# Moving side work between the stages of a tuned decoder step: spatial product, softplus and first units

## The chip, the cores and the metric

The kernel runs on one core of a Trainium2 chip. The metric is the device time of one execution in microseconds (us), the median of several runs. The profile is of one execution; its times are counted from the start of its span.

The engines: TensorE (PE in rows; its weight loads are PEld), VectorE (DVE), ScalarE (ACT), GpSimd (POOL) and SyncE (SP), whose queue issues nearly all transfers (SPq). Each engine does its instructions in the order in which they stand in its queue, and an instruction that waits holds up all behind it.

## The reference

One layer of a gated decoder block for 1024 prompt tokens and 8 sample tokens, model width 1024, float32:

```
h = rmsnorm(x) * (1 + scale) + shift
u, v, g_a, x_b, g_b, z_a, z_b = split(h @ w_in)        # seven blocks of 1024 columns
v = rmsnorm(v) * v_norm_g                               # the sample rows of v are an output
y_a = u * (tril(w_s) @ v + b_s) * silu(g_a)             # in chunks of 128 tokens: the spatial product
xc = causal_conv(x_b)                                   # width 4
r, i = sigmoid(blockdiag(xc) + b)                       # the gates
log_a = -8 * r * softplus(-lam); a = exp(log_a)
y_b = scan(a, sqrt(1 - a*a) * i * xc) * silu(g_b)       # h_t = a h_{t-1} + x_t
out = x + gate * ((sigmoid(z_a) * (y_a @ w_pa) + sigmoid(z_b) * (y_b @ w_pb)) @ w_out)
```

and a last rmsnorm. `softplus(-lam)` is one value per channel, 1024 in all, and does not depend on the input x.

## The kernel before, in words

Each float32 factor is split into a high part (rounded to the matmul format) and a low part, and a product is three matmuls: high by high, high by low, low by high. The high part of a weight is made on ScalarE and the low part on VectorE (`split`).

The work is in four parts. The first makes h and, in tiles of 128 tokens by 512 columns, v (`v_tile`, `v_mm`). `v_evac` copies a v tile out of PSUM on VectorE, squares it on ScalarE for the norm, and stores the copy to DRAM (`vd`). The last tile of v, token block 3 and half 1, is computed after the sums of h that the second part needs (`x_forms`).

The second part is 23 units of seven stages: R (x_b, g_b: recurrent branch), Z (z_a, z_b) and G (u, g_a). The order is R0, Z0, Z1 and then rounds of three, R(i), G(i-1), Z(i+1), and at the end G7. A unit computes two blocks of 128 output columns by seven products (`FORMS` p1 to p7, in the first unit in the order p1, p4, p2, p6, p5, p7, p3), each a stage of 24 matmuls on TensorE (`seven`). The sums of h that they need are made once, and the sums of weights in `sums` on GpSimd. `unit` issues for each stage: the matmuls, the evacuation of the stage before (`evac`, from the list `later`), the weight split two stages ahead (`ahead(.., prep)`), the weight sums four stages ahead (`ahead(.., sums)`), and then the side work that stands in `side` for that stage. In the rows a unit's banks are called `a_R`, `b_R` and so on, its weight halves `wf_R0p`; p1 is copied out to `s_R`, p6 plus p1 to `u_R`.

Side work is put down with `at(stage, function, ...)`: the recurrent branch of unit R(i) (`recurrent`: convolution, gates, scan), and the spatial product for group g (`spatial`): load v, scale it by the norm, split it (`v_hi`, `v_lo`: tiles `vnh`, `vnl`), and two halves of the product (`sp_mm`), each 16 matmuls and, one stage later, its evacuation `fin` on VectorE. `n` in `spatial` is the first stage of G(g), so `n - 4` is the fourth stage of the R unit ahead of it. `do_rgconsts` and `spatial_consts` make small constants between the v tiles and the first unit, the softplus among them.

What sets the order on each queue: the tile framework lists instructions by priority, which is their place in the program, and by when its own model takes them for ready. `tc.high_priority(offset=400)` gives a block the priority of 400 instructions earlier. Where `in_order[0]` is set, every instruction of an engine wrapper (`V`, `A`, `TE`, `G`, `S`) is pinned behind the one traced before it on its engine. It is set for most of the first part and for the units from the second one on; the first unit, R0, is left to the framework's list. `tc.issue_after(x)` pins a block behind the instruction x.

The third part multiplies y_a and y_b by w_pa and w_pb, and the fourth is the product with w_out, the residual and the last norm.

The lines that the change touches: `v_evac` (L668), the sample row's gain (L727), the prefetch in `unit` (L936), the softplus in `do_rgconsts` (L1156 to L1177), the calls ahead of the units (L1440), `spatial` (L1506) and the loop over the units (L1527).

Of the kernel before, what the change touches and what calls it, by code (L numbers as in the profile page):

```python
# [10 lines left out]
AF = mybir.ActivationFunctionType  # L11
ALU = mybir.AluOpType

P = 128
# [10 lines left out]
HD = 512  # L25
# [28 lines left out]
def tile_hybrid_step(  # L54
# [102 lines left out]
        A.activation(hi, src, AF.Copy)  # L157
        (eng or V).tensor_tensor(lo, src, hi.bitcast(F32), ALU.subtract)

    last_w, last_a = [None], [None]  # L160

    def load_raw(name, shape, parts):
        raw = wst[0].tile(shape, F32, tag="raw", name=f"raw_{name}", bufs=4)
# [501 lines left out]
    ssv = ctile([P, NT, 2], "ssv")  # L665
    vd = drm.tile([NP, D], F32, tag="vd", name="vd")

    def v_evac(tt, half, ps):  # L668
        st = half_tile(f"vst{tt}_{half}")[:, 0:HD]
        V.tensor_copy(st, ps)  # L670
        last_a[0] = A.activation(
            junk[:, 0:HD], ps, AF.Square, accum_out=ssv[:, tt, half : half + 1]
        ).ins
        nc.sync.dma_start(out=vd[tt * P : (tt + 1) * P, half * HD : (half + 1) * HD], in_=st)

    vsr = slot("vsr", [P, D])[0:NS]
# [1 line left out]
    def v_tile(tt, half):  # L678
        ps = bank(f"v{tt}_{half}")
        for k in range(KT):  # L680
            if tt < NT:
                ht = h[k, tt // 4]
                tok_mm(ps, (ht[:, 0], ht[:, 1]), wv[k, half], k, P, tok(tt), h0s)
            else:
                packed_mm(ps, hsp, wv[k, half], k, h0s)
        if tt < NT:
            v_evac(tt, half, ps)
        else:
            unpack(vsr[:, half * HD : (half + 1) * HD], ps, NS)

# [33 lines left out]
    with tc.issue_after(last_w[0]):  # L724
        nc.sync.dma_start(out=vgb, in_=v_norm_g[0].partition_broadcast(NS))
    A.activation(vsr, vsr, AF.Copy, scale=rvs)
    V.tensor_tensor(vsr, vsr, vgb, ALU.mult)  # L727
    nc.sync.dma_start(out=chunk_v_sample[0, :, 0, :], in_=vsr)

    for tt in (5, 6, 7):  # L730
# [159 lines left out]
    def ahead(n, step):  # L890
        if n < len(stages):
            step(*stages[n])

    def unit(n0, u, use):
# [33 lines left out]
        for j, f in enumerate(FIRST if first else FORMS):  # L928
            bank_of = {"p1": pa_, "p2": pa_, "p6": pb_, "p7": pb_, "p4": pd_, "p5": pc_, "p3": pc_}
            now = later[:]  # L930
            later.clear()
            seven(u, f, bank_of[f], f in ("p1", "p6", "p5") or (first and f == "p4"))
            for step in now:
                step()
            later.append(lambda f=f: evac(f))
            ahead(n0 + j + 2, prep)  # L936
            ahead(n0 + j + 4, sums)
            for step in side.get(n0 + j, ()):
                step()
# [200 lines left out]
    def do_rgconsts():  # L1140
        pss = consts_pair[:, 1]
        A.activation(sth, pss[:, 0:256], AF.Copy)
        stv = sth[:, 64:256].rearrange("p (b w k) -> p w k b", b=NS, w=3)
        def taps(off):
            return (
                vec[:, off : off + KT].rearrange("p (k o) -> p k o", o=1).broadcast_to([P, KT, NS])
            )

        V.tensor_tensor(pre, stv[:, 0], taps(V_CW), ALU.mult)
        for k in (1, 2):  # L1150
            V.tensor_tensor(stv[:, k], stv[:, k], taps(V_CW + 8 * k), ALU.mult)
        V.tensor_tensor(pre, pre, taps(V_CB), ALU.add)
        for k in (1, 2):
            V.tensor_tensor(pre, pre, stv[:, k], ALU.add)

        lamv = vec[:, V_LAM : V_LAM + KT]  # L1156
        le = ctile([P, KT], "le")
        with tc.issue_after(last_a[0]):
            A.activation(le, lamv, AF.Abs)
        A.activation(le, le, AF.Exp, scale=-1.0)  # L1160
        l1 = ctile([P, KT], "l1")
        V.tensor_scalar(l1, le, 2.0, None, ALU.add)
        V.reciprocal(l1, l1)
        V.tensor_tensor(l1, l1, le, ALU.mult)
        l2 = ctile([P, KT], "l2")
        V.tensor_tensor(l2, l1, l1, ALU.mult)
        l3 = ctile([P, KT], "l3")
        V.tensor_scalar(l3, l2, 1.0 / 15, 1.0 / 13, ALU.mult, ALU.add)
        for n in (11, 9, 7, 5, 3, 1):
            V.tensor_tensor(l3, l3, l2, ALU.mult)  # L1170
            V.tensor_scalar(l3, l3, 1.0 / n, None, ALU.add)
        V.tensor_tensor(l3, l3, l1, ALU.mult)
        V.tensor_scalar(l3, l3, 2.0, None, ALU.mult)
        V.tensor_scalar(l2, lamv, -1.0, 0.0, ALU.mult, ALU.max)
        V.tensor_tensor(l3, l3, l2, ALU.add)
        V.tensor_scalar(crg, l3, C_RG, None, ALU.mult)
        V.tensor_scalar(ncrg, l3, -C_RG, None, ALU.mult)  # L1177

    rgw = {}

# [256 lines left out]
        x_forms(kp)  # L1437
    for n in range(4):
        ahead(n, sums)
    for n in range(2):  # L1440
        ahead(n, prep)
    v_tile(3, 1)
    x_forms(3)
# [54 lines left out]
    def spatial(g, n):  # L1498

        at(n - 9, v_load, g)  # L1500
        at(n - 7, v_mask, g)
        at(n - 7, v_wst, g)
        at(n - 7, v_scale, g)
        at(n - 6, v_hi, g)
        at(n - 5, v_lo, g)
        at(n - 4, sp_mm, g, 0)  # L1506
        at(n - 3, sp_mm, g, 1)

    for i in range(KT):
        recurrent(i)  # L1510
        spatial(i, pos["G", i] + 5 * (i + 1 == KT))
        for step in range(3):
            at(pos["Z", i] + 5 + step, z_late, i, step)
# [10 lines left out]

    users = {"R": use_r, "Z": use_z, "G": use_g}
    for n, u in enumerate(units):
        if n == 1:  # L1527
            in_order[0] = True
        if n + 1 < len(units):
            load_unit(units[n + 1])  # L1530
        unit(7 * n, u, users[u[0]](u[1]))
# [154 lines left out]
```

## Time and profile before

| | |
|---|---|
| three runs | 978.2, 975.4, 978.35 us (median 978.2) |
| the profiled execution | 975.57 us, its span 973.9 us |
| TensorE busy | 940.3 us |
| VectorE busy | 642.0 us |
| ScalarE busy | 499.9 us |
| GpSimd busy | 223.5 us |
| mean granted TensorE clock | 0.996 of full speed |

A busy time is the sum of an engine's instructions. TensorE is the engine that has next to no idle time, so a wait of TensorE is time of the kernel, and work of the other engines matters where TensorE waits for it. A row of a timeline is a run of like instructions: start, length, engine, operation, output and inputs, shapes, count, and in brackets how long the engine stood idle ahead of it and what ended that. The length of a run of matmuls has the fill of the array in it, so one run overlaps the next by some 0.15 us. Nearly all instructions are recorded at line 45, the wrapper that issues them, so tiles and not lines tell them apart.

### The profile page before, as it was taken

The page shows a single profiled execution, that of the slowest core. Times are in us where ns is not written, and L with a number is a line of the kernel's source. Part 1 is how long each engine was busy: PE and PEld are TensorE (multiplying, and loading weights), DVE is VectorE, ACT ScalarE, POOL GpSimd, SP SyncE. Part 2 cuts the span into 40 slices and gives each one's busy share as a digit, 9 for nine tenths or more (in the row PEclk, how much of TensorE's full clock was granted, in tenths as well). Part 3 has the DMA queues.
Part 4 walks back from the last instruction along what each step waited for, and adds up shares of the span by engine and source line. Part 5 has one row for each costly group of instructions (what it writes and reads, how often), then busy time and mean ns, then how long its engine had stood idle before and what let it go on. Part 6 is the DMA issues. An engine that isn't in the chain of part 4 may idle for free. (4 is left out here: it accounts for less than half of the span.)

```text
span 973.9 us, 16564 instructions
## 1 busy us (share of the span) xinstructions
PE 940.3 (97%) x6575; PEld 877.6 (90%) x6575; DVE 642.0 (66%) x973; ACT 499.9 (51%) x809; POOL 223.5 (23%) x169
## 2 busy tenths in 40 slices
PE   7999997999999999999999999999999999999996
PEld 3778777999999999999999999999999999998785
DVE  3886887569578587695784875868534366555544
ACT  4674544684774855846748558467322133232212
POOL 1143432232232243342322433322000000000001
PEclk9999999999999999999999999999999999999999
DMA  9953112143143153241430621607875565424321
GB/s 288 292 169 106 67 36 64 48 141 110 44 139 115 35 165 97 80 152 44 139 93 23 185 69 51 183 23 257 283 271 193 174 213 180 152 93 167 110 71 62
DMA packets 127943, 126.27 MB, mean 130 GB/s; under 512 B 10503, under 2 KB 105279, under 8 KB 127857
## 3 DMA queue, kind: packets, MB, share of 16 engines
q1 hardware_dynamic: 126648, 120.96, 38.9%
q0 software_dynamic: 1216, 4.24, 1.3%
q8 instruction: 52, 0.85, 0.4%
q14 instruction: 27, 0.21, 0.1%
HBM read 93.92 MB, written 31.33 MB: 129 GB/s over the span
## 5 line engine op out<-in xcount | busy, mean ns | idle before, releaser
L45 PE MATMUL v<-wv,h 128*128 128x512 f32 x384 | 97.1, 401 | 2.8 <-ACT junk L45 1.7
L45 PE MATMUL ps_pb<-ybh,pb 128*128 128x344 f32 x384 | 91.0, 320 | 1.0 <-DVE pb L45 0.9
L45 PE MATMUL ps_pa<-yah,pa 128*128 128x344 f32 x384 | 91.4, 320 | 0.0
L45 PEld LDWEIGHTS v<-wv,h 128*128 128x128 f32 x384 | 69.6, 188 | 20.7 <-ACT junk L45 2.2
L45 POOL TENSOR_TENSOR rs_o<-ms_o,nhalf 128x1 f32<-128x1 f32 (+1 forms) x9 | 8.1, 894 | 296.6 <-DVE ms_o L45 296.6
L45 PEld LDWEIGHTS ps_pb<-ybh,pb 128*128 128x128 f32 x384 | 66.2, 188 | 1.5 <-DVE pb L45 1.2
L45 PEld LDWEIGHTS ps_pa<-yah,pa 128*128 128x128 f32 x384 | 66.6, 188 | 0.5
L45 PE MATMUL ps_pb<-ybl,pb 128*128 128x344 f32 x192 | 61.5, 320 | 1.5 <-DVE ybl L45 1.5
L45 PE MATMUL ps_pa<-yal,pa 128*128 128x344 f32 x192 | 61.5, 320 | 0.0
L45 PE MATMUL o<-woh,mgh 128*128 128x512 f32 x128 | 50.5, 395 | 0.0
L45 PE MATMUL o<-woh,mgl 128*128 128x512 f32 x128 | 50.5, 395 | 0.0
L45 PE MATMUL o<-wol,mgh 128*128 128x512 f32 x128 | 50.4, 394 | 0.0
L45 DVE SCALAR_TENSOR_TENSOR xc<-xb,vec,xc 128x512 f32<-128x512 f32 x48 | 48.2, 1005 | 0.6
L45 ACT ACT_TABLE_LOAD x34 | 43.6, 1283 | 1.4 <-PEq L1670 0.8
L45 ACT ACTIVATE mgh<-sa 128x344 fp32r<-128x344 f32 x24 | 11.7, 490 | 63.2 <-DVE sa L45 59.3
L45 DVE TENSOR_TENSOR sb<-ps_pb,sb 128x344 f32<-128x344 f32 x24 | 12.4, 515 | 46.0 <-PE ps_pb L45 46.0
L45 ACT ACTIVATE junk<-xr 128x512 bf16<-128x512 f32 (+2 forms) x19 | 11.6, 608 | 56.8 <-DVE xr L45 51.4
L45 POOL TENSOR_TENSOR wt_R<-raw_R,raw_R 128x512 f32<-128x512 f32 x8 | 16.9, 2106 | 95.4 <-DVE wf_Z5p L45 13.7
L45 PEld LDWEIGHTS ps_pb<-ybl,pb 128*128 128x128 f32 x192 | 36.0, 188 | 2.1 <-DVE ybl L45 2.1
L45 PEld LDWEIGHTS ps_pa<-yal,pa 128*128 128x128 f32 x192 | 36.1, 188 | 0.2
L45 POOL TENSOR_TENSOR wt_G<-raw_G,raw_G 128x512 f32<-128x512 f32 x8 | 14.0, 1755 | 92.9 <-DVE wf_G6p L45 13.9
L45 POOL TENSOR_TENSOR wt_R<-raw_R,wt_R 128x512 f32<-128x512 f32 x15 | 33.1, 2207 | 8.6 <-DVE wf_R6p L45 1.1
(535 smaller groups left out, 2543.3 us busy)
## 6 DMA issues: line engine op xcount, KB each, us to landing
raw_ada<-in_w_ada_dram SPq DMA_DIRECT2D x32, 256.0 KB
raw_R<-in_w_in_dram SPq DMA_DIRECT2D x16, 512.0 KB
raw_Z<-in_w_in_dram SPq DMA_DIRECT2D x16, 512.0 KB
raw_G<-in_w_in_dram SPq DMA_DIRECT2D x16, 512.0 KB
zad<-za SPq DMA_DIRECT2D x16, 258.0 KB
yad<-t SPq DMA_DIRECT2D x8, 516.0 KB
sb<-zbd SPq DMA_DIRECT2D x8, 516.0 KB
yar<-yad SPq DMA_DIRECT2D x8, 516.0 KB
```

What stands on the lines that cost most here:

```text
L45: ins = f(*args, **kwargs)
```

## The change

The spatial product's two halves go from stages n - 4 and n - 3 to n - 3 and n - 2, and with them their evacuations. The softplus is taken out of `do_rgconsts` and put down as side work in five pieces: its ScalarE operations, with a Sigmoid on a scratch tile behind them, in the first unit's third stage, and four groups of VectorE operations in stages 10 to 13, which are the last four of Z0. `in_order` is set from the first unit on. The weight split of R0's third stage is put ahead of the last v tile. The evacuations in `v_tile` get the priority of 400 instructions earlier. The product of the sample row of v with its gain goes from VectorE to GpSimd.

```diff
@@ -157,7 +157,7 @@
         A.activation(hi, src, AF.Copy)
         (eng or V).tensor_tensor(lo, src, hi.bitcast(F32), ALU.subtract)
 
-    last_w, last_a = [None], [None]
+    last_w = [None]
 
     def load_raw(name, shape, parts):
         raw = wst[0].tile(shape, F32, tag="raw", name=f"raw_{name}", bufs=4)
@@ -665,12 +665,11 @@
     ssv = ctile([P, NT, 2], "ssv")
     vd = drm.tile([NP, D], F32, tag="vd", name="vd")
 
-    def v_evac(tt, half, ps):
+    def v_evac(tt, half, ps, late=False):
         st = half_tile(f"vst{tt}_{half}")[:, 0:HD]
-        V.tensor_copy(st, ps)
-        last_a[0] = A.activation(
-            junk[:, 0:HD], ps, AF.Square, accum_out=ssv[:, tt, half : half + 1]
-        ).ins
+        with tc.high_priority(offset=400 if late else 0):
+            V.tensor_copy(st, ps)
+            A.activation(junk[:, 0:HD], ps, AF.Square, accum_out=ssv[:, tt, half : half + 1])
         nc.sync.dma_start(out=vd[tt * P : (tt + 1) * P, half * HD : (half + 1) * HD], in_=st)
 
     vsr = slot("vsr", [P, D])[0:NS]
@@ -684,7 +683,7 @@
             else:
                 packed_mm(ps, hsp, wv[k, half], k, h0s)
         if tt < NT:
-            v_evac(tt, half, ps)
+            v_evac(tt, half, ps, True)
         else:
             unpack(vsr[:, half * HD : (half + 1) * HD], ps, NS)
 
@@ -724,7 +723,7 @@
     with tc.issue_after(last_w[0]):
         nc.sync.dma_start(out=vgb, in_=v_norm_g[0].partition_broadcast(NS))
     A.activation(vsr, vsr, AF.Copy, scale=rvs)
-    V.tensor_tensor(vsr, vsr, vgb, ALU.mult)
+    G.tensor_tensor(vsr, vsr, vgb, ALU.mult)
     nc.sync.dma_start(out=chunk_v_sample[0, :, 0, :], in_=vsr)
 
     for tt in (5, 6, 7):
@@ -933,7 +932,8 @@
             for step in now:
                 step()
             later.append(lambda f=f: evac(f))
-            ahead(n0 + j + 2, prep)
+            if n0 + j > 0:
+                ahead(n0 + j + 2, prep)
             ahead(n0 + j + 4, sums)
             for step in side.get(n0 + j, ()):
                 step()
@@ -1153,28 +1153,31 @@
         for k in (1, 2):
             V.tensor_tensor(pre, pre, stv[:, k], ALU.add)
 
-        lamv = vec[:, V_LAM : V_LAM + KT]
-        le = ctile([P, KT], "le")
-        with tc.issue_after(last_a[0]):
+    lamv = vec[:, V_LAM : V_LAM + KT]
+    le, l1, l2, l3 = (ctile([P, KT], n) for n in ("le", "l1", "l2", "l3"))
+
+    def softplus(step):
+        if step < 0:
             A.activation(le, lamv, AF.Abs)
-        A.activation(le, le, AF.Exp, scale=-1.0)
-        l1 = ctile([P, KT], "l1")
-        V.tensor_scalar(l1, le, 2.0, None, ALU.add)
-        V.reciprocal(l1, l1)
-        V.tensor_tensor(l1, l1, le, ALU.mult)
-        l2 = ctile([P, KT], "l2")
-        V.tensor_tensor(l2, l1, l1, ALU.mult)
-        l3 = ctile([P, KT], "l3")
-        V.tensor_scalar(l3, l2, 1.0 / 15, 1.0 / 13, ALU.mult, ALU.add)
-        for n in (11, 9, 7, 5, 3, 1):
-            V.tensor_tensor(l3, l3, l2, ALU.mult)
-            V.tensor_scalar(l3, l3, 1.0 / n, None, ALU.add)
-        V.tensor_tensor(l3, l3, l1, ALU.mult)
-        V.tensor_scalar(l3, l3, 2.0, None, ALU.mult)
-        V.tensor_scalar(l2, lamv, -1.0, 0.0, ALU.mult, ALU.max)
-        V.tensor_tensor(l3, l3, l2, ALU.add)
-        V.tensor_scalar(crg, l3, C_RG, None, ALU.mult)
-        V.tensor_scalar(ncrg, l3, -C_RG, None, ALU.mult)
+            A.activation(le, le, AF.Exp, scale=-1.0)
+            A.activation(pre_act, nhalf, AF.Sigmoid)
+        elif step == 0:
+            V.tensor_scalar(l1, le, 2.0, None, ALU.add)
+            V.reciprocal(l1, l1)
+            V.tensor_tensor(l1, l1, le, ALU.mult)
+            V.tensor_tensor(l2, l1, l1, ALU.mult)
+            V.tensor_scalar(l3, l2, 1.0 / 15, 1.0 / 13, ALU.mult, ALU.add)
+        elif step < 3:
+            for n in ((11, 9, 7), (5, 3, 1))[step - 1]:
+                V.tensor_tensor(l3, l3, l2, ALU.mult)
+                V.tensor_scalar(l3, l3, 1.0 / n, None, ALU.add)
+        else:
+            V.tensor_tensor(l3, l3, l1, ALU.mult)
+            V.tensor_scalar(l3, l3, 2.0, None, ALU.mult)
+            V.tensor_scalar(l2, lamv, -1.0, 0.0, ALU.mult, ALU.max)
+            V.tensor_tensor(l3, l3, l2, ALU.add)
+            V.tensor_scalar(crg, l3, C_RG, None, ALU.mult)
+            V.tensor_scalar(ncrg, l3, -C_RG, None, ALU.mult)
 
     rgw = {}
 
@@ -1437,7 +1440,7 @@
         x_forms(kp)
     for n in range(4):
         ahead(n, sums)
-    for n in range(2):
+    for n in range(3):
         ahead(n, prep)
     v_tile(3, 1)
     x_forms(3)
@@ -1503,9 +1506,12 @@
         at(n - 7, v_scale, g)
         at(n - 6, v_hi, g)
         at(n - 5, v_lo, g)
-        at(n - 4, sp_mm, g, 0)
-        at(n - 3, sp_mm, g, 1)
-
+        at(n - 3, sp_mm, g, 0)
+        at(n - 2, sp_mm, g, 1)
+
+    at(2, softplus, -1)
+    for step in range(4):
+        at(10 + step, softplus, step)
     for i in range(KT):
         recurrent(i)
         spatial(i, pos["G", i] + 5 * (i + 1 == KT))
@@ -1524,7 +1530,7 @@
 
     users = {"R": use_r, "Z": use_z, "G": use_g}
     for n, u in enumerate(units):
-        if n == 1:
+        if n == 0:
             in_order[0] = True
         if n + 1 < len(units):
             load_unit(units[n + 1])
```

## Rows read from the trace of the kernel before

**Rows 1.** the page: busy time of each engine, share of the span, instructions

```profile
PE 940.3 (97%) x6575; PEld 877.6 (90%) x6575; DVE 642.0 (66%) x973; ACT 499.9 (51%) x809; POOL 223.5 (23%) x169
```

**Rows 2.** waits of TensorE: in total, times, longest (us)

```profile
PE sp L45 <- DVE vnl L45: 9.7, 7, 1.4
...
PE b_R L45 <- ACT u_R L45: 3.7, 1, 3.7
```

**Rows 3.** timeline of TensorE, last v tile to Z0: start, us, what

```profile
136.95 5.85 PE L45 MATMUL v<-wv,h 128*128 128x512 f32 x24 [1.73 <-ACT junk L45]
...
143.97 3.12 PE L45 MATMUL a_R<-h,wf_R0p 128*128 128x258 f32 x24
...
151.62 3.13 PE L45 MATMUL a_R<-h,wf_R0p 128*128 128x258 f32 x24 [1.65 <-ACT s_R L45]
...
164.16 4.58 PE L45 MATMUL b_R<-S,wf_R0p 128*128 128x258 f32 x24 [3.70 <-ACT u_R L45]
...
168.58 3.03 PE L45 MATMUL c_R<-S,wf_R0p 128*128 128x258 f32 x24
...
171.45 3.03 PE L45 MATMUL a_Z<-h,wf_Z0p 128*128 128x258 f32 x24
```

**Rows 4.** stretches: busy (x count) by engine, granted clock, DMA share, GB/s

```profile
164.00:166.00 2.00, 1.84 (x8) 1.84 (x9) 1.42 (x3) 1.11 (x3) 0.00 (x0) 0.50 0.29 84
...
196.00:198.00 2.00, 2.00 (x19) 2.00 (x18) 0.69 (x1) 2.00 (x4) 0.00 (x0) 1.00 0.32 122
```

**Rows 5.** timeline of VectorE, last v tiles and R0

```profile
127.48 4.89 DVE L45 TENSOR_TENSOR vsr<-vsr,vgb 8x1024 f32<-8x1024 f32 x1 [1.64 <-ACT vsr L45]
...
152.41 0.17 DVE L45 TENSOR_SCALAR l<-le 128x8 f32<-128x8 f32 x1
...
158.74 0.16 DVE L45 TENSOR_SCALAR ncrg<-l 128x8 f32<-128x8 f32 x1
...
162.78 0.69 DVE L45 TENSOR_TENSOR b_R<-b_R,s_R 128x516 f32<-128x516 f32 x1
```

**Rows 6.** timeline of GpSimd, last v tiles and R0

```profile
126.24 3.80 POOL L45 TENSOR_TENSOR f<-h 128x516 f32<-128x516 f32 x3
...
130.01 1.28 POOL L45 TENSOR_TENSOR wt<-raw_R,wt_R 128x512 f32<-128x512 f32 x1
...
150.58 1.72 POOL L45 TENSOR_TENSOR rs_v<-ms_v,nhalf 128x8 f32<-128x8 f32 x1 [9.71 <-DVE ms_v L45]
```

**Rows 7.** timeline of VectorE, units R3 and G2

```profile
357.43 1.22 DVE L45 TENSOR_TENSOR vnl<-vg,vnh 128x1024 fp32r<-128x1024 f32 x1
...
359.75 0.75 DVE L45 SCALAR_TENSOR_TENSOR t<-sp,vgc,wsr 128x512 f32<-128x512 f32 x1 [0.50 <-PE sp L45]
...
371.79 0.68 DVE L45 TENSOR_TENSOR wf_G2p<-wt_G,wf_G2p 128x512 fp32r<-128x512 f32 x1
```

**Rows 8.** timeline of ScalarE, R0

```profile
149.58 1.28 ACT L45 ACT_TABLE_LOAD   x1
...
150.99 0.58 ACT L45 ACTIVATE s_R<-a_R 128x516 f32<-128x516 f32 x1
```

**Rows 9.** timeline of the SP queue: transfers issued

```profile
145.87 2.52 SPq L45 DMA_DIRECT2D rgw<-in_w_rg_x_dram  x4
...
190.33 1.14 SPq L45 DMA_DIRECT2D raw_R<-in_w_in_dram  x2
```

**Rows 10.** timeline of TensorE, units R3 and G2

```profile
357.03 0.28 PE L45 MATMUL sp<-wsb,vnh 128*128 128x256 f32 x1
...
359.55 3.09 PE L45 MATMUL b_R<-S,wf_R3p 128*128 128x258 f32 x24
...
362.48 0.29 PE L45 MATMUL sp<-wsb,vnh 128*128 128x256 f32 x1
...
363.35 3.09 PE L45 MATMUL c_R<-S,wf_R3p 128*128 128x258 f32 x24
...
374.88 3.02 PE L45 MATMUL c_G<-S,wf_G2p 128*128 128x258 f32 x24
```

## The prediction

> **What bounds the kernel now.** I read the page's busy times first. TensorE is busy for 940.3 of the 973.9 us [rows 1], so what a reordering can give is in the 34 us in which it is not, and in stretches where its clock is low. The list of TensorE's waits comes next: one group, the spatial product waiting for the low part of v (`vnl`), has 9.7 us in 7 waits of up to 1.4, and the longest single wait is 3.7 us for the copy `u_R` [rows 2]. The timeline of TensorE at the first unit shows where the others lie: 1.73 us ahead of the last v tile, 1.65 us ahead of R0's third stage, and the 3.70 us ahead of its sixth [rows 3]. The windows then show what the long one costs besides: right behind it the granted clock is 0.50, the lower level (1.2 of 2.4 GHz), where it was 1.00 [rows 4].
>
> Everything the change touches is in these two places. Waits are priced from start to start, because a matmul's row also has the fill of the pipe in it and an idle array must be filled again.
>
> **The first unit.** From the start of p1 (143.97) to the start of Z0 (171.45) R0's seven stages take 27.48 us [rows 3]. An undisturbed stage takes 171.45 - 168.58 = 2.87 us, so seven take 20.1. The difference, 7.4, is the two waits (5.35), 1.55 from the sixth stage at the low clock (4.42 from 164.16 to 168.58, less 2.87), and refilling. With the 1.73 ahead of the v tile there is 9.1 us to be had. What ends each wait:
>
> - 1.73: the v tile takes the banks of an earlier v tile, whose evacuation is behind VectorE's product of the sample row with the gain, 4.89 us long [rows 5]. It ended at 132.37, 1.08 after GpSimd's run of sums ended (131.29) [rows 6]; the low part `vnl`, as long a row on 128 partitions, takes 1.22 [rows 7]. So 3.7 of the 4.89 was waiting for GpSimd. The change takes the product off VectorE, and the priority of 400 puts the copy and the square of a late v tile ahead of the sums of h (`x_forms`). On GpSimd the product costs about 2.5: three sums of 516 took 3.80 [rows 6], 1.27 each, and it has 1024. Its upper bound is the 4.89 it took on VectorE, its lower one the 1.22. I take 2.5, scaled from its own engine. Behind it on GpSimd are one to three form sums and `wt4`; these end at some 134 in place of 131.3, and their first reader that TensorE needs is p4's weight, at 145. It is hidden; without that cover it would cost its 2.5 once.
> - 1.65: ScalarE did the softplus's table load (1.28 at 149.58) before the copy `s_R` (150.99) [rows 8], though p1 had ended by 147.1. In program order `s_R` comes behind p4's matmuls and ahead of the softplus, so it can go right when p1 ends, 3 us before p2 asks.
> - 3.70 and the clock: the sum `b_R + s_R` ran at 162.78, though p5 had ended at 160.46 (164.16 less the 3.70) and p6 a stage ahead of it, by 157.6. VectorE first did the rest of the 23 small softplus operations, which run from 152.41 to 158.90 [rows 5], and then weight halves and convolution taps. In program order the sum stands behind one weight half.
>
> What is late next, in the new order: TensorE starts p1 at 142.2, then p4 at 145.2, p2 148.1, p6 150.9, p5 153.8, p7 156.7, Z0 162.4. ScalarE has, behind p4's end (148.1): a copy and a weight half to 149.3, then the softplus head with two table loads (one for Exp, one to preload Sigmoid). A load and the Exp behind it take 1.41 until `s_R` starts [rows 8], so the head is over by 152.4. Then p2's copies, p7's weight half (ends 153.8), its low part on VectorE (0.68 [rows 7]) to 154.5, the sum of p6 (0.69 [rows 5]) to 155.2, the copy `u_R` to 155.8. p7 asks at 156.7: 0.9 us to spare, the tightest place of the unit.
>
> The new pins add waits too. VectorE's first operation of unit 0 must follow the copy of the v norms, which waits for GpSimd's power, 1.72 [rows 6]; that hangs on the square of the last v tile, now near 142.8 (135.2 + 5.9 for the tile, 0.7 each for the copy and the square and a little more), so the norms' copy is done near 145. Behind it is p6's weight half, which p6 needs at 150.9: 4 us of cover at least. GpSimd's sum for p7's weight, once made early, is now pinned behind that power: ready near 146.4, wanted near 153. On SP the load of Z0's weights, earlier issued far ahead, is now pinned behind R0's eight small gate loads, whose last four ended issuing at 148.4 [rows 9]. Two loads of 512 KB each issued at 190.33 took 1.14 to issue, and the transfers had thinned out to 0.32 by 196 to 198 [rows 4, 9]; so Z0's weights land by some 156, and its first half is wanted on ScalarE at about 157.4, on TensorE at 162.4. Covered by 4 us against TensorE. The four softplus steps on VectorE lie in Z0's last four stages, 6.5 / 23 x 6 = 1.7 us each at most by the rows, and end a stage ahead of the tanh that reads them; TensorE shows no wait in that stretch. The weight half of p2 is prepared ahead of the last v tile and no more in stage 0: the same two operations, earlier.
>
> For the unit: 9.1, lower bound 0 (the waits only change names), upper bound 9.1.
>
> At the table loads the trace and a rule part. By the rows a switch is paid with 1.41, Exp included. The Trainium skill, "ScalarE: Activation LUTs", section "What ACT_TABLE_LOAD costs", gives about 2.66 us for every switch, a drain of about 1.38 behind the load. The two switches would by that be 2.5 us dearer, p7 would wait about 1.6, and the gain of the unit would be about 7.5; the row does not show such a drain, so I go by the row.
>
> **The rounds.** In R3, the round I take for all seven, the first spatial product starts at 357.03 and the stage behind it at 359.55, 2.52 us later; the second one takes 363.35 - 362.48 = 0.87 [rows 10]. So the wait costs 1.65 a round, a little more than the 1.40 that is listed, and 7 x 1.65 = 11.5 us. `vnl` is ready at 358.65 [rows 7]. One stage later the product comes behind p7, at 357.03 + 2.87 = 359.9: 1.25 us after `vnl`, and TensorE does not wait.
>
> What moves with it on VectorE: the two evacuations of the product, four operations of 0.75 [rows 7] and a short one, 3.2 us a round, each one stage later, into the stages with the convolution. Their readers, the G unit's products, are two stages off or more; in the last unit too, where the first half is used one stage after it is written. VectorE has no gap from 359.75 to the weight half that ends at 372.47, and p5 of G starts at 374.88 [rows 7, 10]: 2.41 to spare. TensorE now comes 1.65 earlier, and VectorE gets back the half microsecond that it stood idle ahead of the first evacuation, so some 1.3 us is left. I cost the move at nothing; if that cover is gone, up to 3.0 a round. At the end of the last G the second evacuation falls in front of the scan's inputs; that is between nothing and 1.5 us, and I take nothing, as in the rounds.
>
> **Sum.** 9.1 + 11.5 = 20.6 us. The profiled execution took 975.57 us, 1.67 over its span: 975.57 - 20.6 = 955.0. The three runs are 978.2, 975.4 and 978.35, so the median lies 2.6 above the profiled one; for the median of the new kernel I add half of that: 956.3.
>
> **The rivals.**
>
> - First unit: the waits change their names. The pinned queues put each engine's work behind whatever waits longest (the norms' copy on VectorE, the softplus head on ScalarE), and TensorE stands about as long as before at p6 or p7. Only the 1.73 stays: 956.3 + 7.4 = 963.7. For it: 0.9 us to spare at p7. Against: VectorE is freed of the 4.89 and of most of the 6.5 in this stretch.
> - The priority and the move to GpSimd change nothing at the v tile, because another operation is put first. 956.3 + 1.7 = 958.0.
> - Dear table loads hold up `u_R`: if each of the two switches kept ScalarE for twice the load's 1.28 [rows 8], that is 2.6 more, less the 0.9 to spare: 956.3 + 1.7 = 958.0. Against it is the 1.41 to `s_R`. The section of the Trainium skill on ScalarE named above speaks for it.
> - VectorE becomes late in the rounds: all 3.0 us of moved work fall ahead of p5's weight half, which had 1.3 to spare. A wait of 1.7 a round takes the place of the 1.65; the rounds give nothing: 956.3 + 11.9 = 968.2.
> - Slower: the same VectorE paces the stretch, the 3.0 us come through in full, and the clock falls in each round as it did behind the 3.70 (it stayed at 1.00 at the waits of 1.4). 3.0 + 1.55 = 4.55 a round, 31.9 in all: 956.3 + 31.9 = 988.2. It decides at 20.6 / 7 = 2.9 us of loss a round. The unbroken VectorE stretch speaks for it, the 1.3 us against it.
> - Neither place gains, since something untraced holds TensorE: about 976.
>
> **How the numbers follow.** Chances: forecast 0.60, v tile 0.07, table loads 0.03, first unit 0.14, rounds 0.10, slower 0.03, nothing 0.03. The likeliest case alone: 953.5 to 959. The range: down to 952.5, if runs sit at the profiled level (955.0) and the last G gives another 1.5 or a little more; up to 967, which takes in the unit's rival and most of the rounds' one. About 0.3% (2.9 us) is what can be told from no change here. Slower by more: 0.03; within: 0.03; faster: 0.94.
>
> **What would show it.** After: the list of TensorE's waits has neither `sp` for `vnl` nor `a_R` and `b_R` in R0; the granted clock is 1.00 in R0; p1 of R0 to Z0 takes about 20.2 us; a round from one R to the next is 1.65 shorter. Wrong steps would show as waits of R0 for `u_R` or a weight half, of p5 in G for a weight half, of the gate matmuls for the convolution's halves, or of the last v tile for the square. The forecast fails if any of these repeats in seven rounds.

## The result, and the profile after

The changed kernel takes 968.31 us (median of 965.57, 968.35, 968.27 and 968.96), the kernel before it, run beside it, 976.82 (four runs, 975.4 to 978.35): ratio 0.9907, 95% interval [0.9879, 0.9935]. It is faster by 8.5 us and not by 20.6; 956.3 was forecast, and 968.31 lies outside the range of 952.5 to 967. The profiled execution took 965.57 us, the least of the four, and its span went from 973.9 to 963.9.

Start to start on TensorE, the 10.0 us divide as follows (v3 is the last v tile; R0, Z0, R1, ..., G7 are the first products of those units):

| stretch | before | after | gain | forecast |
|---|---|---|---|---|
| start to v3 | 136.95 | 137.00 | -0.05 | 1.7 |
| v3 to Z0 | 34.50 | 28.60 | 5.90 | 7.4 |
| Z0 to R1 | 42.34 | 46.45 | -4.11 | 0 |
| R1 to G7 | 441.13 | 433.16 | 7.97 | 11.5 |
| G7 to the end | 318.98 | 318.69 | 0.29 | 0 |

The list of TensorE's waits in the changed kernel (us in total, times, longest) answers to [rows 2]:

```profile
PE psc L45 <- ACT crow L45: 3.6, 1, 3.6
PE ps_pb L45 <- issue: 2.8, 1, 2.8
PE v L45 <- ACT junk L45: 2.1, 1, 2.1
PE b_Z L45 <- DVE p_Z L45: 2.1, 1, 2.1
...
PE b_R L45 <- DVE wf_R0p L45: 0.5, 1, 0.5
PE a_R L45 <- ACT s_R L45: 0.4, 1, 0.4
PE b_G L45 <- DVE wf_G3p L45: 0.2, 1, 0.2
```

The spatial product's 9.7 and the 3.70 are gone. The wait of `psc` is at the very start, which the change does not touch (3.4 before). Three more waits of over 2 us stand there: the v tile's, one of Z0 that is new, and one ahead of the output phase. In TensorE's timeline they read (last v tile, R0's third stage and the stage that waited for a weight half, then Z0's last stage):

```profile
137.00 5.85 PE L45 MATMUL v<-wv,h 128*128 128x512 f32 x24 [2.09 <-ACT junk L45]
...
144.01 3.12 PE L45 MATMUL a_R<-h,wf_R0p 128*128 128x258 f32 x24
...
150.37 3.13 PE L45 MATMUL a_R<-h,wf_R0p 128*128 128x258 f32 x24 [0.35 <-ACT s_R L45]
...
154.21 2.93 PE L45 MATMUL b_R<-S,wf_R0p 128*128 128x258 f32 x22 [0.47 <-DVE wf_R0p L45]
...
186.99 4.65 PE L45 MATMUL b_Z<-h,wf_Z0p 128*128 128x258 f32 x24 [2.08 <-DVE p_Z L45]
```

R0 takes 21.59 us from p1 to Z0 where [rows 3] had 27.48. Z0's last stage takes 4.65 instead of some 3.0: behind its wait the granted clock is low (0.50 from 188 to 190 us), as it was in [rows 4].

**Why Z0 waits.** VectorE and then GpSimd of the changed kernel in that stretch (start, us):

```profile
182.05 0.16 DVE L45 TENSOR_TENSOR l<-l,l 128x8 f32<-128x8 f32 x1
182.25 1.28 DVE L45 TENSOR_SCALAR l<-l 128x8 f32<-128x8 f32 x1
183.56 0.17 DVE L45 TENSOR_TENSOR l<-l,l 128x8 f32<-128x8 f32 x1
183.76 1.16 DVE L45 TENSOR_SCALAR l<-l 128x8 f32<-128x8 f32 x1
184.95 1.18 DVE L45 TENSOR_TENSOR l<-l,l 128x8 f32<-128x8 f32 x1
...
186.25 0.69 DVE L45 TENSOR_TENSOR p_Z<-b_Z,p_Z 128x516 f32<-128x516 f32 x1
```

```profile
182.21 1.28 POOL L45 TENSOR_TENSOR wt_Z<-raw_Z,raw_Z 128x512 f32<-128x512 f32 x1 [14.19 <-DVE l L45]
183.58 1.31 POOL L45 TENSOR_TENSOR wt_Z<-raw_Z,wt_Z 128x512 f32<-128x512 f32 x1
184.85 1.25 POOL L45 TENSOR_TENSOR raw_Z<-raw_Z 128x512 f32<-128x512 f32 x1
```

Three softplus operations of 8 columns, 0.17 us each elsewhere, take 1.16 to 1.28, and each ends with one of GpSimd's three sums. The 3.1 us that this adds stand ahead of `p_Z`, for which TensorE waits. The Trainium skill, "SBUF — State Buffer", section "Who interferes with whom", says that VectorE and GpSimd share one pair of ports, which one instruction holds until it ends, and that an operation with two operands in SBUF, or some with one, needs it. These rows agree. `p_Z` has one operand in PSUM; here it runs when the sums are over, but in the run a2 below it overlaps one, and both take their usual 0.69 and 1.28.

**Why the v tile still waits.** VectorE, then GpSimd, of the changed kernel; they answer to [rows 5] and [rows 6]:

```profile
130.86 3.49 DVE L45 TENSOR_TENSOR f<-f,f 128x516 f32<-128x516 f32 x2 [4.73 <-POOL vsr L45]
...
135.48 0.68 DVE L45 COPY vst<-v 128x512 f32<-128x512 f32 x1
```

```profile
125.93 2.55 POOL L45 TENSOR_TENSOR f<-h 128x516 f32<-128x516 f32 x2
128.44 2.38 POOL L45 TENSOR_TENSOR vsr<-vsr,vgb 8x1024 f32<-8x1024 f32 x1
130.79 1.29 POOL L45 TENSOR_TENSOR f<-h 128x516 f32<-128x516 f32 x1
```

VectorE stood idle for 4.73 until GpSimd's product ended, and the copy that frees v3's bank comes at 135.48, behind four sums as before. The raised priority moved nothing: with the offset at 0 the program has the same instructions in the same order on all five engines.

**Why the rounds give half.** TensorE, then VectorE, in G2; they answer to [rows 10] and [rows 7]:

```profile
372.67 3.03 PE L45 MATMUL a_G<-h,wf_G2p 128*128 128x258 f32 x24
...
376.06 0.50 PE L45 MATMUL b_G<-S,wf_G2p 128*128 128x258 f32 x2
376.79 2.90 PE L45 MATMUL b_G<-S,wf_G2p 128*128 128x258 f32 x22 [0.23 <-DVE wf_G2p L45]
```

```profile
373.02 1.23 DVE L45 TENSOR_TENSOR xe<-xc,xe 64x1032 fp32r<-64x1032 f32 x1 [1.06 <-ACT xe L45]
374.17 0.69 DVE L45 TENSOR_TENSOR b_G<-b_G,s_G 128x516 f32<-128x516 f32 x1
...
376.04 0.69 DVE L45 TENSOR_TENSOR wf_G2p<-raw_G,wf_G2p 128x512 fp32r<-128x512 f32 x1 [1.19 <-ACT wf_G2p L45]
```

The product of G's fifth stage waits for its weight half, at the end of a chain over VectorE and ScalarE. (From the second unit on, the order of the products is p1, p6, p5, p2, p7, p3, p4, so this is p7.) The wait is listed with 0.23; since the stage is cut in two by it, it costs more: from the `rg` product ahead of the stage to the one behind it TensorE takes 4.23, and 3.35 before. These 0.88 are what is missing of the 1.65. Rounds 1 to 4 are 0.78 us shorter than before, rounds 5 and 6, which have no subtraction `y_lo` on VectorE, 1.82 and 1.72.

### The profile page after: what moved, and what is told of

Same layout as the page of the kernel before. It is cut to its first block, busy times and chain, and to the rows that moved or that the text cites. A ratio compares the mean times of both kernels' runs of the same rounds, so it can differ in the third digit from the quotient of the medians.

```text
span 963.9 us, 16594 instructions
## 1 busy us (share of the span) xinstructions
PE 940.5 (98%) x6575; PEld 878.1 (91%) x6575; DVE 645.2 (67%) x972; ACT 499.7 (52%) x810; POOL 228.1 (24%) x170
## 5 line engine op out<-in xcount | busy, mean ns | idle before, releaser
L45 POOL TENSOR_TENSOR rs_o<-ms_o,nhalf 128x1 f32<-128x1 f32 (+1 forms) x9 | 8.0, 894 | 296.3 <-DVE ms_o L45 296.3
L45 DVE SCALAR_TENSOR_TENSOR xc<-xb,vec,xc 128x512 f32<-128x512 f32 x48 | 50.3, 1049 | 0.6
L45 POOL TENSOR_TENSOR wt_Z<-raw_Z,raw_Z 128x512 f32<-128x512 f32 x8 | 10.8, 1351 | 98.9 <-DVE l L45 14.2
```

The costliest lines, as they stand in the source:

```text
L45: ins = f(*args, **kwargs)
```

## The experiments

Each run is the changed kernel with one edit, if nothing else is said. What they measured (the waits and stretches from each one's own profile, us; the median and ratio against the kernel before from its timed runs):

| run | wait v3 | v3-Z0 | Z0-Z1 | R1-R5 | R5-G7 | G7-pb | span | median | ratio |
|---|---|---|---|---|---|---|---|---|---|
| before | 1.7 | 34.50 | 22.26 | 263.37 | 177.76 | 22.54 | 973.9 | | |
| after | 2.1 | 28.60 | 26.36 | 260.26 | 172.90 | 24.88 | 963.9 | 968.31 | 0.9907 |
| a1_sp_back | 2.1 | 28.71 | 26.37 | 263.12 | 177.68 | 22.24 | 972.9 | 975.17 | 0.9980 |
| a2_soft_bunch | 2.1 | 28.61 | 22.68 | 260.66 | 172.89 | 24.87 | 962.4 | 964.34 | 0.9872 |
| a3_ylo_31 | 2.1 | 28.72 | 26.36 | 260.98 | 173.05 | 24.87 | 965.4 | 967.09 | 0.9892 |
| a4_vsr_behind | 2.4 | 28.60 | 26.37 | 260.23 | 172.89 | 24.87 | 964.2 | 966.29 | 0.9896 |
| b1_soft_early | 2.1 | 28.57 | 23.91 | 260.16 | 172.99 | 24.86 | 964.1 | 965.60 | 0.9884 |
| b3_unit0_free | 2.1 | 29.87 | 24.62 | 260.18 | 172.97 | 24.87 | 963.3 | 966.01 | 0.9895 |
| c1_ylo_out | 2.1 | 28.73 | 26.35 | 256.80 | 172.89 | 24.86 | 962.5 | 964.63 | 0.9877 |
| c2_prep_first | 2.1 | 28.61 | 26.35 | 261.08 | 173.14 | 25.98 | 970.5 | 970.30 | 0.9937 |
| d0_vgb_own | 1.6 | 28.58 | 26.36 | 260.12 | 172.86 | 24.89 | 964.3 | 965.52 | 0.9877 |
| d3_both | 1.5 | 28.59 | 22.70 | 260.62 | 172.90 | 24.90 | 962.8 | 964.02 | 0.9863 |
| d2_three | 1.6 | 28.55 | 22.73 | 261.74 | 173.00 | 24.90 | 963.4 | 964.52 | 0.9872 |
| d4_ylo_pool | 0.9 | 28.56 | 22.69 | 261.64 | 172.90 | 24.89 | 963.4 | 964.70 | 0.9866 |
| e1_vsr_back | 1.7 | 28.62 | 26.35 | 260.20 | 172.95 | 24.86 | 967.9 | 967.69 | 0.9912 |
| g1_other_bank | 2.1 | 28.73 | 26.32 | 260.25 | 172.96 | 21.92 | 964.6 | 966.22 | 0.9906 |
| g2_best | 1.5 | 28.54 | 22.72 | 260.53 | 172.87 | 21.94 | 960.8 | 962.48 | 0.9864 |

The intervals are 0.0011 to 0.0020 either way (0.0028 for the changed kernel), so most ratios of neighbours overlap; the stretches, which repeat to 0.2 us where an edit does not reach, tell the edits apart. The table leaves out the time ahead of v3 and behind `ps_pb`, which differs by up to 3 us from one profile to the next, so a span by itself says little.

### Is the later spatial product what the rounds gained?

```
-        at(n - 3, sp_mm, g, 0)
-        at(n - 2, sp_mm, g, 1)
+        at(n - 4, sp_mm, g, 0)
+        at(n - 3, sp_mm, g, 1)
```

> The changed kernel with the spatial product back one stage earlier; all else as changed. Theory (the later product is worth what the starts of the R units show, 0.78 a round in rounds 1 to 4 and 1.3 to 1.8 in rounds 5 to 7, 8.0 us up to the start of G7): the waits of TensorE for vnl come back, 7 of about 1.4, and the time is 7.5 to 8.5 us above the changed kernel, about 1 to 2 us under the kernel before. Rival (the rounds gain nothing by it and the first unit is what made the kernel faster): the time stays within 2 us of the changed kernel.

975.17 us, ratio 0.998 [0.9969, 0.9992]: 6.9 above the changed kernel, a little less than the 7.5 to 8.5 expected. `sp` waits for `vnl` again, 9.5 us in 7, and R1 to G7 takes 440.80. The later product is worth those 7.6 us, most of what the change brings on balance; without it some 2 us are left by the timed runs.

### Where do rounds 1 to 4 lose the other half?

c1 leaves the operation out, a3, d2 and d4 put it elsewhere, c2 makes G's fifth weight half ahead of the evacuations:

```
 def y_lo(i):            # c1: left out; d4 (upon d3): G. for V.
-    V.tensor_tensor(gr[:].bitcast(F32R), gr, scan_out[i], ALU.subtract)
...
-            at(n + 25, y_lo, i)
+            at(n + 31, y_lo, i)         # a3; n + 32 in d2 (upon d3)
...
+            prep_first = u[0] == "G" and j == 2      # c2
+            if prep_first:
+                ahead(n0 + j + 2, prep)
             for step in now:
                 step()
```

> The changed kernel with the low part of y_b (1.23 us on VectorE in rounds 1 to 4) six stages later, behind the weight half of p7 of G. Theory (in rounds 1 to 4 VectorE's chain up to the weight half of p7 in G, which had 0.9 us to spare before, takes back 0.84 of the 1.65; rounds 5 to 7 have no such operation): the four waits of 0.2 for wf_G go, rounds 1 to 4 become as short as rounds 5 to 7, and the time is about 3.4 us under the changed kernel. Rival (ScalarE's order, the copy u_G and the convolution's halves, sets p7 whatever VectorE does ahead of it): no change, within 1 us.

> The changed kernel without VectorE's subtraction for the low part of y_b in groups 0 to 3 (the stored low part is then the whole y_b); only that operation of 1.23 us a round is left out. Theory (VectorE's queue from the product's evacuation to the gates paces rounds 1 to 4): with 1.23 us less in it, rounds 1 to 4 are as short as rounds 5 and 6, so each gains 0.8 to 1.0, 3.3 to 4 us in all, and the waits for wf_G and for the gates' bank are gone. Rival (ScalarE's place in the chain, u_G ahead of the weight half of p7, paces them): less than 1 us in all.

> The changed kernel with the weight split of G's fifth product issued ahead of the evacuation of its second (so ScalarE makes the weight half before the copy u_G, and VectorE the low part before the sum of b_G). Theory (the 0.2 waits in G, 0.84 us a round from start to start, are the fifth weight half standing behind a chain convolution, xe, b_G, u_G): the waits for wf_G go and rounds 1 to 4 gain up to 0.84 each, 3.4 in all, unless the gates' halves, now behind the weight half, become late: then a wait at rg takes part of it back, and 1 to 2 us remain. Rival (VectorE's load as such): the same time is lost at the next product, and nothing is gained.

> As d3_both, and the subtraction y_lo seven stages later (at n + 32 instead of n + 25), one stage behind the place tried before, where VectorE's t for the spatial product stood behind it. Theory (any place hurts that stands ahead of an operation for which TensorE waits; stage n + 32 is behind t): rounds 1 to 4 take 64.2 us as with the subtraction left out, R1 to R5 256.9, 3.4 less than d3_both: span about 957. Rival (VectorE is full from the G units on): another operation comes late by the same 1.2 us, and R1 to R5 stays at 259.5 to 261.

> As d3_both, and the subtraction y_lo at its old stage (n + 25) but on GpSimd. Theory (load): VectorE has 1.2 us less in front of the G unit's fifth weight half, rounds 1 to 4 take 64.2 us, span about 957. Rival (shared port): GpSimd's subtraction of 1.3 us holds up the VectorE operation beside it as its sums held up the small softplus operations, and rounds 1 to 4 take 64.8 to 65.2.

Without the subtraction R1 to R5 takes 256.80, 3.46 us less, each round 64.1 to 64.3 as rounds 5 and 6 do: this one operation on VectorE costs the other half. Moving it gains nothing. The waits that each gives TensorE in place of those for G's weight half, from a3, c2 and d2 in this order:

```profile
PE rg L45 <- DVE t L45: 3.0, 4, 0.9
```

```profile
PE rg L45 <- DVE t L45: 2.3, 4, 0.6
```

```profile
PE b_G L45 <- DVE t L45: 3.9, 4, 1.2
```

`t` is the evacuation that now stands behind the moved work. On GpSimd (d4) the subtraction takes 2.93, and a tap of the convolution (`xc`) beside it takes 2.89 on VectorE, until it is over. The same tap takes 1.77 in the changed kernel, beside a shorter sum, and 0.75 where none runs:

```profile
356.46 2.93 POOL L45 TENSOR_TENSOR gr<-gr,th 128x1032 fp32r<-128x1032 f32 x1
```

```profile
357.04 2.89 DVE L45 SCALAR_TENSOR_TENSOR xc<-xb,vec,xc 128x512 f32<-128x512 f32 x1
```

R1 to R5 stays at 260.98, 261.08, 261.74 and 261.64 (a3, c2, d2, d4), so the theories of all four failed. In a3, c2 and d2 the waits for G's weight half do go, against a3's rival on ScalarE, and a wait for another VectorE operation comes instead: VectorE is full from the G units on. In d4 the waits for the weight half stay, and rounds 1 to 4 take 65.4 to 65.5, more than even the rival on the port had. (c2 is slower as a whole, 0.9937. Its span is 6.6 us longer: 1.1 in the rounds, 1.1 in G7, which waits 0.7 for `t`, 1.9 behind the start of `ps_pb`, at a granted clock of 0.57 in the first 4 us, and 2.6 ahead of v3, where its edit does not reach; these 2.6 stay open.)

### Does GpSimd hold up the softplus?

```
     for step in range(4):
-        at(10 + step, softplus, step)
+        at(10 if step < 3 else 13, softplus, step)      # a2
```

> The changed kernel with the first three VectorE groups of the softplus (17 operations) all in stage 10, ahead of the weight half behind which GpSimd's sums start; the fourth stays in stage 13. Theory A (VectorE's small operations are held up one GpSimd operation each while GpSimd makes the sums for Z1; their number costs little): each takes about 0.2, no operation of 1.2; the wait of Z0's last stage for p_Z falls from 2.08 to 0.4 or less, its clock stays at 1.00, and Z0 to Z1 takes about 3.3 us less than the 26.4 of the changed kernel. Theory B (it is the number of operations put in front of p_Z): all 17 now stand ahead of it, and the wait is 2 us or more.

> The changed kernel with the whole softplus (ScalarE and VectorE) right behind the load of its input, in the first part, where VectorE and ScalarE have idle time and TensorE runs v products. Theory (the softplus among Z0's stages costs the wait of 2.08 for p_Z, 1.6 of low clock behind it and some 0.5 around; elsewhere it is free): Z0 to Z1 takes 22.3 in place of 26.4, as before the change, and R0 is at least as short; about 4 us under the changed kernel. Rival (Z0 waits because the unit comes 6 us earlier, for its weights or for the gates, and the softplus only happens to stand there): Z0's wait stays or goes over to another operand.

VectorE of a2: 17 operations, of which the first and the last are shown, and what follows; then the first of GpSimd's sums.

```profile
180.74 0.16 DVE L45 TENSOR_SCALAR l<-le 128x8 f32<-128x8 f32 x1
...
184.02 0.17 DVE L45 TENSOR_SCALAR l<-l 128x8 f32<-128x8 f32 x1
184.10 0.69 DVE L45 TENSOR_TENSOR wf_Z0p<-wt_Z,wf_Z0p 128x512 fp32r<-128x512 f32 x1
184.71 0.69 DVE L45 TENSOR_TENSOR p_Z<-b_Z,p_Z 128x516 f32<-128x516 f32 x1
```

```profile
184.87 1.28 POOL L45 TENSOR_TENSOR wt_Z<-raw_Z,raw_Z 128x512 f32<-128x512 f32 x1 [16.22 <-DVE wf_Z0p L45]
```

More operations in one stage, none beside a sum, none longer than 0.20: Z0 to Z1 falls from 26.36 to 22.68, and the wait for `p_Z` is gone. Theory A held: GpSimd's hold on the ports and not the count of operations was the price. With the whole softplus earlier (b1) the wait goes too, but the gates then load Sigmoid's table, 1.28 us, and `rg` waits 1.4: 23.91 and not the 22.3 expected. Three of its operations meet GpSimd there as well (1.19 to 1.26), and of the 4 us expected the medians show 2.7 and the spans none.

### What would free the last v tile?

a4 puts the product behind GpSimd's sums for `x_forms`, d0 holds `vgb` elsewhere, d3 adds a2's edit to d0, e1 takes the product back to VectorE:

```
-    vgb = slot("vgb", [P, D])[0:NS]                          # d0, d3
+    vgb = aux[0].tile([P, D], F32, tag="x", name="vgb", bufs=2)[0:NS]
...
-    G.tensor_tensor(vsr, vsr, vgb, ALU.mult)
+    V.tensor_tensor(vsr, vsr, vgb, ALU.mult)                 # e1
```

> The changed kernel with GpSimd's product of the sample row behind the last of its sums for x_forms in place of ahead of it. Theory (the wait ahead of the last v tile stayed because VectorE's sums, ahead of the copy of the tile before, now stand until GpSimd is done with the product and the last sum): the sums start at 128.5 to 130 in place of 130.9, the copy ends by some 134, the wait of 2.1 falls to 0.7 or less, and Z0 starts 1.5 us or more earlier against the start of the wait. Rival (the copy is late by VectorE's own work, whatever GpSimd does): the wait stays within 0.5 of 2.1.

> The changed kernel, but the sample row's scale vgb is held in a tile that the x rows no longer need, and not in a slot of the ring from which the Strassen sums take theirs. Theory (buffer): VectorE's first sum of pair 2 writes into the slot that held vgb, so it waited for GpSimd's product with vgb, wherever that stood on GpSimd. With vgb elsewhere it waits for GpSimd's sums alone, the copy of v6 comes 2 us or more earlier, the wait of 2.1 us ahead of the last v tile falls below 0.4, and as VectorE's chain begins earlier too, the stretch from the last v tile to Z0 stays at 28.6: span 963.9 - 2 = about 962. Rival (sums): VectorE waited for GpSimd's sums; the wait stays 2.0 to 2.4. Rival (chain): the wait goes but the stretch to Z0 grows by 2, and the span stays at 963.5 to 964.3.

> As the kernel before this one of the call (vgb out of the ring), and softplus steps 0 to 2 together at stage 10, ahead of GpSimd's sums. If the two gains lie in different stretches they add: Z0 to Z1 at 22.7 instead of 26.4, and the last v tile at 135, span about 960 (962.4 with softplus alone, less 2). If one is given back by the other, the span is 961.5 to 962.5.

> The changed kernel with the sample row's product back on VectorE, nothing else. Theory (the move is worth nothing): the product on VectorE stands behind GpSimd's three sums as before (about 4.9 us), the copy of v6 ends within 0.3 us of where it ended, the wait of the last v tile stays at 1.7 to 2.1, span 963.5 to 964.3. Rival (the move was worth its 1.7): the wait is larger by 1 to 2 and the span 965 or more.

In a4 the product is the last of the four on GpSimd, VectorE still starts only at its end, and the wait is 2.4 and not under 0.7. The slots show why: VectorE's first sum of pair 2 takes the slot that held `vgb`, so its semaphore wait names the product. In d0 that is gone, and the wait has another cause (VectorE, then GpSimd):

```profile
126.81 5.88 DVE L45 TENSOR_TENSOR f<-f,f 128x516 f32<-128x516 f32 x2 [1.73 <-POOL f L45]
...
134.91 0.68 DVE L45 COPY vst<-v 128x512 f32<-128x512 f32 x1
```

```profile
125.47 3.83 POOL L45 TENSOR_TENSOR f<-h 128x516 f32<-128x516 f32 x3
129.27 2.86 POOL L45 TENSOR_TENSOR vsr<-vsr,vgb 8x1024 f32<-8x1024 f32 x1
```

VectorE starts 4 us sooner and stands inside its two sums, 5.88 for 1.40 of work, until 0.56 after GpSimd's product. The copy comes 0.57 earlier, the wait is 1.6 and not under 0.4: the buffer was a cause, and behind it the shared port was the next. How long VectorE stands is not the same each time: d4 has the same code here, its two sums took 3.52, the two behind them 2.28 and 1.78, and the wait was 0.9. The spans expected of d0 and d3, 962 and 960, were missed with 964.3 and 962.8; behind `ps_pb`, as shown below for d3, the granted clock fell.

With the product on VectorE (e1) it takes 4.89 as in [rows 5], the wait is 1.7, and from v3 to G7 the run takes 508.21 us, as the changed kernel does. So the move to GpSimd is worth nothing; it makes the wait 0.36 longer. The span of e1, 967.9, lies outside what its theory and its rival had: 1.5 of the 4.0 us above the changed kernel lie ahead of v3, and 2.5 behind `ps_pb`, at a clock of 0.50 in its first 4 us; timed, the two are alike (967.69 and 968.31).

### What does program order do in the first unit?

```
-        if n == 0:
+        if n == 1:
             in_order[0] = True
```

> The changed kernel with the first unit left to the framework's list again (program order from Z0 on); the softplus stays side work. Theory (most of the 5.9 us that R0 gained came from taking the softplus out of the way, the program order adds the rest): in the new list the convolution's first two taps stand ahead of the sum b_R + s_R, so the wait for u_R comes back with 1 to 2.5 us and R0 takes 22.5 to 24.5 us, between the 27.5 of before and the 21.6 of the changed kernel. Rival 1 (program order is all): 26 or more. Rival 2 (the softplus is all): 21.6 within 0.3.

v3 to Z0 takes 29.87, with waits of 1.1 for `s_R` and 1.1 for `u_R`. Of the 5.90 program order gives 1.3. The rest, 4.6, comes without it; that it is the softplus gone from that place is argued, no run put it back there.

The softplus was not all that stood ahead of `b_R + s_R` in the kernel before. Two taps of the convolution did too, beside GpSimd's sums, and took 3.44 where two take 1.5 elsewhere (VectorE, then the first of the two sums):

```profile
159.42 3.44 DVE L45 SCALAR_TENSOR_TENSOR xc<-xb,vec,xc 128x512 f32<-128x512 f32 x2
```

```profile
158.88 1.76 POOL L45 TENSOR_TENSOR wt_Z<-raw_Z,wt_Z 128x512 f32<-128x512 f32 x1
```

By these rows some 1.9 of the 3.70 us for `u_R` came of the same hold-up as in Z0. In b3 the two taps stand there again, with 3.47; program order puts the sum ahead of them.

b3 shows one thing more: behind the same wait of 2.1 for `p_Z` its clock stayed at 1.00, and Z0 to Z1 took 24.62. So 1.7 of the 4.1 that Z0 lost is the low clock, and the wait need not bring it.

### What happened ahead of the output phase?

```
     new_phase()
+    for j in range(4):
+        V.memset(bank(f"skip{j}")[:, 0:1], 0.0)
```

> The changed kernel, but the output phase begins in other banks: VectorE clears one column of the phase's first four, so that the first product ps_pb takes the fifth, which lies over a pair that has long been read out. Theory (bank): TensorE waited 2.8 ahead of ps_pb for VectorE's t<-b_G,t, as the first bank lies over the pair of b_G; with the other bank ps_pb starts 2.5 to 2.8 sooner after G7, waits then in pieces for the split of pb and the last ybl (2.0 to 2.4 together, as in the kernel before), and the span is 963.5, since VectorE's end is what sets both. Rival (the wait itself): nothing behind it waits again, and the span falls to 961. Rival (not the bank): the single wait of 2.8 stays.

> As d3_both (vgb out of the ring of slots, softplus steps 0 to 2 together) and the output phase in the other banks. d3_both started ps_pb 3.6 us before the changed kernel in its own time and ended only 1.1 before it, with the granted clock at 0.50 and 0.73 in the first 8 us of ps_pb. Theory (clock behind the single wait): with the wait in pieces the clock stays at 1.00 there, and the span is 962.8 - 2.5 = about 960. Rival (clock falls anyway): 962 to 963.

In the changed kernel the phase's first bank lies over the pair of `b_G`, which VectorE reads out last. In other banks (g1) TensorE starts `ps_pb` 2.96 us sooner after G7 and then stands 2.4 in pieces (g2's are the same):

```profile
PE ps_pb L45 <- DVE ybl L45: 1.7, 2, 1.1
...
PE ps_pb L45 <- DVE pb L45: 0.7, 1, 0.7
```

g1 as a whole gains nothing (0.9906, span 964.6): what VectorE has still to deliver, `pb` and `ybl`, sets that place. What the wait in one piece can cost shows in d3, in stretches of 4 us from `ps_pb` on (busy by engine, granted clock, DMA share, GB/s):

```profile
666.00:670.00 4.00, 3.46 (x12) 3.49 (x13) 3.93 (x5) 2.24 (x3) 0.00 (x0) 0.50 1.02 295
670.00:674.00 4.00, 4.00 (x20) 4.00 (x19) 3.81 (x5) 2.74 (x3) 0.00 (x0) 0.66 1.10 374
```

and in g2, which is d3 with the other banks:

```profile
664.00:668.00 4.00, 3.26 (x21) 2.89 (x19) 3.97 (x10) 0.00 (x0) 0.00 (x0) 1.00 0.39 113
668.00:672.00 4.00, 2.33 (x14) 1.85 (x13) 3.99 (x7) 3.78 (x4) 0.00 (x0) 1.00 1.11 346
```

d3 came to `ps_pb` 3.55 us before the changed kernel and ended only 1.1 before it. g2 ends 3.1 before it: 962.48 us, ratio 0.9864 [0.9851, 0.9878], where the changed kernel has [0.9879, 0.9935] and g1, timed beside it, 966.22 us. It has the lowest median and span of all versions. d3's ratio is the same, 0.9863: that the banks add to it is seen in the spans, 962.8 and 960.8, and not in the timed runs.

## Why the prediction was wrong, by its steps

- **"The change takes the product off VectorE" (1.7).** Failed: v3 starts no earlier and its wait is 2.09 in place of 1.73. GpSimd's 2.5 was right (2.38), but not that "it is hidden": VectorE waited for it, 4.73 us, by the slot; and with that slot free (d0) it stood beside it, by the port. I had read from [rows 5, 6] that 3.7 of the 4.89 was waiting for GpSimd, and did not ask what the next VectorE operation would do beside the same run. The priority was taken at its word; it moves nothing. This is the rival on the v tile.
- **The first unit (7.4).** Right in kind: no wait for `u_R`, clock 1.00, 21.59 us against 20.2. p7, my tightest place, did not wait; p6 did, by 0.47, where I had 4 us of cover. p6's weight half stood behind the copy of the v norms, which was expected near 145, came at 151.73 and took 1.30 beside a GpSimd sum, not the 0.17 of an operation of 8 columns. It came late since VectorE copied the last v tile out only at 148.05, behind the sums of `x_forms` as before (148.00), and not right behind the tile. I also put all of the 3.70 down to what stood ahead of the sum on VectorE, and did not see that GpSimd had stretched the two taps there. The table loads went by the row, as the prediction took them:

```profile
153.47 1.28 ACT L45 ACT_TABLE_LOAD   x1
154.76 0.20 ACT L45 ACTIVATE pre_act<-nhalf 128x2 f32<-128x2 f32 x1
```

- **The softplus steps, "1.7 us each at most ... TensorE shows no wait in that stretch" (0).** The step that failed worst: step 1 took 4.3 us, the wait was 2.08, and with the clock behind it Z0 lost 4.1. The bound came from a stretch in which GpSimd stood idle from 152.30 to 157.49; one operation of the 23 met a sum there (`crg` at 157.68, 1.16 us), and that warning I read past. I did not lay GpSimd's sums of Z0 beside the new place. No rival held it.
- **The rounds (11.5).** The term of 1.65 was right where VectorE has room (1.82 and 1.72) and mis-sized in rounds 1 to 4 (0.78). I had found 2.41 to spare at p5; p7 of G had 0.9, and I did not read it. The rival "VectorE becomes late in the rounds" named the cause, with the wrong place and size: p5 and 1.7 a round in all seven, where it was p7 and 0.88 in four.
- **The last G ("between nothing and 1.5, I take nothing").** Right in the sum: 0.29. TensorE lost 2.3 ahead of `ps_pb` and got 2.6 back behind it, as the waits in pieces of before went. That the two cancel was luck: the prediction has nothing on the banks of the next part, and where the clock fell behind the wait, as in nine other runs, less came back.

Together 1.75 + 1.5 + 4.1 + 3.5 are missing and 0.3 was found: a gain of 10.0 in the profile, 10.6 less than the 20.6. The forecast of the median was off by 12.0; the other 1.4 is that the median lies 2.7 above the profiled execution, where 1.3 had been added.

## What to carry to other kernels

Before work is moved to a place where VectorE "has room", lay GpSimd's instructions of that place beside it: an operation of 0.17 us with its operands in SBUF cost here what was left of the GpSimd instruction that it met, 1.16 to 1.30 us, once for each. When a wait is taken away, look for the tightest reader over the whole round and not at the first one that fits, and for the buffer that the moved instruction's operands hand on. A wait for a semaphore that is removed can come back as a longer instruction.

## What had not been expected of the hardware

Behind a single wait of 2.8 to 3.0 us ahead of `ps_pb` the granted clock of the next 4 us was 0.50 to 0.65 in nine of the thirteen profiled executions that had it, and 1.00 in four, the changed kernel's among them; in the four with the wait in pieces it stayed at 1.00. From `ps_pb` to the end the nine took 295.0 to 296.3 us and the four 293.3 to 293.8, so the fall cost 1.2 to 3.0 us, as much as most of the edits are worth. The changed kernel's profile is one without it; whether its three slower executions, with a mean granted clock of 0.991 to 0.993 and not 0.995, had it, no trace shows. Behind the wait of 2.1 for `p_Z` the clock fell in nine of ten (0.57 to 0.68 over the next 4 us), and stayed at 1.00 in b3. Behind the v tile's 2.1 to 2.4 it fell in five runs of ten (a1, a3, a4, c1, g1: the tile and the small products behind it took 8.4 to 8.6 instead of 7.0) at no cost: R0 was then free of its two small waits, and v3 to Z0 took 28.6 to 28.7 all the same. What decides between the two outcomes, these runs do not show.
